# Squares and block sums of the first three groups of an MLP's first product: in halves, in one stretch, and in other places

## The chip, the cores and the metric

The kernel runs on one core of one Trainium2 chip. The metric is the device time of one execution in microseconds. Engines are named as in the profile: PE (TensorE, the matrix engine), DVE (VectorE), ACT (ScalarE), POOL (GpSimd) and SP (SyncE, which issues the DMAs here). Each engine works through its own instructions strictly in the order in which the program issued them; where one waits, all behind it wait.

## The reference

One pre-norm encoder block over 1024 tokens of width 1024. What matters here is its last part:

```
h = rms_norm(x, norm2_g) @ w_mlp_in          # 1024 -> 4096
x = x + square(relu(h)) @ w_mlp_out          # 4096 -> 1024
```

Ahead of it stand an input projection, neighbourhood attention, a gated short convolution and an output projection. All are float32.

## The kernel before, in words

Every float32 operand is split into a scaled float16 high part and a float16 low part, and every product is done in three passes (high x high, high x low, low x high). The larger products are done by Winograd's form of Strassen's method: of two 2x2 block matrices, seven block products instead of eight, with sums of blocks before and behind.

The first MLP product is cut into 16 *groups* (q = 0 to 15). A group takes 256 of the 4096 hidden columns, as two blocks of 128, and all 1024 tokens, as two blocks of 512; its result is a 2x2 of blocks of 128 partitions x 512. `quad(q, c0, c1)` does one group for the columns c0 to c1 of the 512. Groups 0 and 1 are done in halves, since the tokens of the second half (256 to 511) are normalized later: the order is `quad(0, 0, 256)`, `quad(1, 0, 256)`, `quad(0, 256, 512)`, `quad(1, 256, 512)`, then whole groups from 2 on.

A group is seven *units*, one for each block product, of 12 matmuls each (4 slices of the contraction x 3 passes). The order of the products is 1, 6, 5, 4, 2, 7, 3, and in the second halves 1, 2, 5, 4, 6, 7, 3. Each product goes to one of eight PSUM banks in turn. The tile `as` of a group has seven places z[0] to z[6] of 128 x 512 float32 and there are two such tiles, so group q + 2 reuses the tile of group q. What is done with the products ("sums of products"):

- product 1: ACT copies it to z[4] (L1475)
- product 6: z[5] = product 6 + z[4] on DVE (L1458)
- product 5: z[1] = product 5 - z[5] (L1463)
- product 2: z[0] = product 2 + z[4] (L1477)
- product 7: z[6], z[2], z[3] from products 7, 4 and 5 (L1466 to L1468)
- product 3: z[1] = product 3 + z[1] (L1471)

z[0] to z[3] are then the four blocks of h. `h_done(q)` finishes the group: ReLU on ACT over z[0:4] in place (L1432), scaled square in place with its maximum bound accumulated (L1434), four *block sums* by `sums` for the second MLP product (z[5], z[2], z[4], z[6] from z[0] to z[3]; L1159; on DVE for groups 0 and 1, on POOL from group 2 on), and the store of the whole tile to DRAM (L1438, queue `hs`). When the store has been issued, the group leaves `live`; `quad(q + 2)` steps the foreground until it has.

The order of the work on the engines is written out by the program as it is built, with generators. `unit` issues a unit's matmuls, then the sums of products of the unit *before* it (`settle`), and then advances generators: each `step()` advances every generator in the foreground list `fg` by one `yield`, each `tick()` the first one in the background list `bg`. A unit of a first half makes three steps, every other unit two, and each makes five ticks. `h_done(q)` is put into `fg` with the sums of product 3, so its first advance stands behind the first unit of the next group.

In the background the weights of the groups to come are prepared, one group after the other: rows scaled on ACT (L952), squares on ACT (L961), sums of blocks on POOL (L966); then, some units later, a sum over the squares and its cast on DVE (L932, L933), a one-column matmul with a matrix of ones on PE (L179), the scale from it on DVE (L182, L405 to L412), and the split into high parts on ACT (L981) and low parts on DVE (L977). For group q + 2 the one-column matmul stands behind the fourth unit of group q, and the splits behind its sixth.

`forms_m` splits the weights of group 1 by hand and puts parts of them where room is left; two of the places are the tiles `t2` and `t4` of 128 x 2 x 512 float16, read by group 1's products 6 and 4.

Of the kernel before, what the change touches and what calls it, by code (L numbers as in the profile page):

```python
# [10 lines left out]
F32 = mybir.dt.float32  # L11
# [3 lines left out]
AF = mybir.ActivationFunctionType  # L15
# [37 lines left out]
def encoder_block(ctx: ExitStack, tc: tile.TileContext, x, weights, cols, gqk, rel, masks, out):  # L53
    nc = tc.nc
    V, A, G, T, SP = nc.vector, nc.scalar, nc.gpsimd, nc.tensor, nc.sync
# [23 lines left out]
    sc = base.tile([128, 512], F32, name="sc")  # L79
# [3 lines left out]
    def cols_of(kind, n):  # L83
        a = area[kind]
        if a[1] + n > a[2]:
            assert kind != "keep"
            a[1] = a[0]
        a[1] += n
        return slice(a[1] - n, a[1])

    def keep(n=1):
        return cols_of("keep", n)

    def tmp(n=1):
        return cols_of("tmp", n)

    def at(c, i, n=1):
        return slice(c.start + i, c.start + i + n)
# [6 lines left out]
    def pow2(mx, top, s, inv, floor=True, more=0):  # L105

        if floor:
            V.tensor_scalar(sc[:, mx], sc[:, mx], 1e-30, None, op0=OP.max)
            yield
        V.tensor_scalar(sci[:, inv], sci[:, mx], EXP, None, op0=OP.bitwise_and)  # L110
        yield
        V.tensor_scalar(sci[:, s], sci[:, inv], -1.0, float((254 + top) << 23), op0=OP.mult, op1=OP.add)
        V.tensor_scalar(sci[:, inv], sci[:, inv], 1.0, float(-(top + more) * (1 << 23)), op0=OP.mult, op1=OP.add)
        yield


    fg, bg = [], []
# [9 lines left out]
    def step(n=1):  # L127
        for _ in range(n):
            for g in list(fg):
                if not advance(g):  # L130
                    fg.remove(g)
# [80 lines left out]
    def load_upto(n):  # L212
        while loaded[0] < min(n - held[0], limit[0], len(loads)):
            ch, p = loads[loaded[0]]
            loaded[0] += 1
            t = rawp.tile([128, 1024], F32, name="raw")
            load_into(t[:, :ch.widths[p][0] * ch.widths[p][1]], ch, p)
            ch.raw.append(t)
# [107 lines left out]
    for (kind, j), pieces in plan():  # L326
# [4 lines left out]
        for p, (k, w) in enumerate(ch.widths):  # L331
            ch.offs.append(offset)
            if kind != "X" and (kind, j) != ("1", 0) and (kind, j, p) != ("1", 1, 1):
# [3 lines left out]
    cV, cConv, cA, cB, cO, c1, c2, c2x = ([chunks[k, j] for j in range(n)] for k, n in  # L337
                                              (("V", 2), ("C", 4), ("A", 4), ("B", 4), ("O", 2),
                                               ("1", 16), ("2", 4), ("X", 4)))
# [205 lines left out]
    for p in range(11):  # L545
# [7 lines left out]
        for q in (p,) if p < 6 else (2 * p - 6, 2 * p - 5):  # L553
            c = q // 2 + 3
# [306 lines left out]
    for k in range(N + 15):  # L861
        p, w = k // 16, k % 16
# [147 lines left out]
    def seven(P, act, c0, c1, posts, steps, ticks, order=(1, 6, 5, 4, 2, 7, 3)):  # L1010

        ps = {}
        at_w = P if callable(P) else lambda w, i, k: P[:, w, i, k * 128:k * 128 + 128]
        for i in order:
            f, w = SEVEN[i]
            ps[i] = anybank()[:, c0:c1]
            post = posts.get(i)
            unit(group(ps[i], [(at_w(w, sw, k), act(f, sa, k)[:, c0:c1])
                               for k in range(4) for sw, sa in PASSES]),
                 post and (lambda post=post: post(ps)), steps, ticks)  # L1020
# [134 lines left out]
    def sums(f, sub):  # L1155

        z = [f[:, i] for i in range(7)]
        for o, a, b, op in ((5, 0, 2, OP.subtract), (2, 2, 3, OP.subtract), (4, 2, 0, OP.subtract), (6, 1, 4, OP.add)):
            sub.tensor_tensor(z[o], z[a], z[b], op=op)  # L1159
            yield  # L1160
# [27 lines left out]

    PART = ((0, 4), (4, 7))

    spare = []

    def pieces(n, part):

# [30 lines left out]
    def need(i):  # L1225
        while i not in ready:
            assert bg
            forced[0] = True
            tick()
            step()  # L1230
        forced[0] = False
# [51 lines left out]
    def forms_m():  # L1283

        (w11, w12), (w21, w22) = ([c1[1].raw[i].rearrange("p (n m) -> p n m", n=2)[:, j] for j in range(2)]
                                  for i in range(2))
        s = scaled[0]
        three = [rawp.tile([128, 1024], F32, name="raw").bitcast(F16).rearrange("p (f i c) -> p f i c", f=2, i=2)
                 for _ in range(3)]
        spare.extend(three[:2])  # L1290
        two = three[2]
        held[0], limit[0] = 3, c1[2].first + 1
        load_upto(done[0] + 5)
        t2 = w4p.tile([128, 2, 512], F16, name="t2", bufs=1)
        t4 = w4p.tile([128, 2, 512], F16, name="t4", bufs=1)
        k4 = lambda v: v.rearrange("p (k c) -> p k c", k=4)
        flat = {0: lambda i: P1[0][:, 7, i], 1: lambda i: two[:, 0, i], 2: lambda i: two[:, 1, i],
                5: lambda i: t2[:, i], 6: lambda i: t4[:, i]}

        def place(f, i):  # L1300
            return k4(flat[f](i)) if f in flat else M[0][:, 4 * (f - 3):4 * (f - 3) + 4, 512 * i:512 * i + 128]

        P1[1] = lambda f, i, k: place(f, i)[:, k]
        src = {0: w11, 1: w21, 2: w22, 3: w11, 4: w12, 5: w22, 6: w21}

        def hi(f):
            A.activation(place(f, 0), k4(src[f]), AF.Copy, scale=sc[:, s])

        def lo(f):
            V.scalar_tensor_tensor(place(f, 1), k4(src[f]), sc[:, s], place(f, 0), op0=OP.mult, op1=OP.subtract)  # L1310

        def add(o, a, b):
            V.tensor_tensor(o, a, b, op=OP.add)

        hi(0), hi(2), hi(1), lo(0), add(w11, w11, w12), lo(2)
        yield
        add(w12, w12, w22)
        yield
        add(w22, w22, w11), lo(1), hi(5), add(w21, w21, w22), hi(6)
        yield  # L1320
        lo(5), lo(6)
        yield
        hi(3), hi(4)
        yield
        lo(3)
        yield
        lo(4)
        done[0] += 1
        held[0], limit[0] = 1, c1[3].first
        load_upto(done[0] + 5)  # L1330
        ready.add(1)
# [16 lines left out]
    def wait(n):  # L1348
        for _ in range(n):
            yield  # L1350
# [17 lines left out]
    def tail(b, half, *acts):  # L1368
        proj(b, half, acts)
        for a in acts:  # L1370
            a()

    chain = forms_m()

    def sq(b, half=None):
# [48 lines left out]


    AS, live = {}, set()
    bsum, R = [keep(4) for _ in range(4)], [(keep(), keep()) for _ in range(4)]
    r_ready = [False] * 4

    def h_done(q):  # L1430
        f = AS.pop(q)
        A.activation(f[:, 0:4], f[:, 0:4], AF.Relu)  # L1432
        yield
        A.activation(f[:, 0:4], f[:, 0:4], AF.Square, scale=sc[:, c1[q].inv],  # L1434
                     accum_out=sc[:, at(bsum[q // 4], q % 4)])
        yield
        yield from sums(f, G if q > 1 else V)
        SP.dma_start(HS[q // 4][:, :, q % 4], f)  # L1438
        live.remove(q)
        if q % 4 == 3:  # L1440
            m = tmp()
            V.tensor_reduce(sc[:, m], sc[:, bsum[q // 4]], axis=AX, op=OP.max)
            yield
            yield from pow2(m, 14, *R[q // 4])
            r_ready[q // 4] = True

    def quad(q, c0=0, c1=512):
        need(q)
        if c0 == 0:
            while q - 2 in live:  # L1450
                step()
            live.add(q)
            AS[q] = w4p.tile([128, 7, 512], F32, name="as", tag="as")
        ps = {}
        z = [AS[q][:, i, c0:c1] for i in range(7)]

        def post6(ps):
            V.tensor_tensor(z[5], ps[6], z[4], op=OP.add)  # L1458
            if c0:
                post5(ps)  # L1460

        def post5(ps):
            V.tensor_tensor(z[1], ps[5], z[5], op=OP.subtract)  # L1463

        def post7(ps):
            V.tensor_tensor(z[6], ps[7], z[5], op=OP.add)  # L1466
            V.tensor_tensor(z[2], ps[4], z[6], op=OP.add)  # L1467
            V.tensor_tensor(z[3], ps[5], z[6], op=OP.subtract)  # L1468

        def post3(ps):  # L1470
            V.tensor_tensor(z[1], ps[3], z[1], op=OP.add)  # L1471
            if c1 == 512:
                fg.append(h_done(q))
        seven(P1[q], actU2, c0, c1, {
            1: lambda ps: A.activation(z[4], ps[1], AF.Copy),  # L1475
            6: post6, 5: None if c0 else post5,
            2: lambda ps: V.tensor_tensor(z[0], ps[2], z[4], op=OP.add),  # L1477
            7: post7, 3: post3}, 2 if c1 == 512 else 3, 5, (1, 2, 5, 4, 6, 7, 3) if c0 else (1, 6, 5, 4, 2, 7, 3))

    def whole(q):  # L1480
        quad(q)
        pe_done[0] = q + 1

    quad(0, 0, 256)
    quad(1, 0, 256)
    while pair_done[0] < 4:
        step()
# [131 lines left out]
    t2 = w5p.tile([128, 2, 1024], F32, name="t2")  # L1619
# [119 lines left out]
```

## Time and profile before

| | before |
|---|---|
| median of 3 timed runs | 1243.88 us (1243.17 to 1244.32) |
| profiled execution | 1241.45 us, span 1239.7 us |
| PE busy | 1200.9 us, 97% of the span |
| DVE, ACT, POOL busy | 930.0 (75%), 765.2 (62%), 425.5 us (34%) |
| granted TensorE clock, mean | 0.996 |
| first MLP product | from 645.75 us of the span |

The profile is of one execution. Its timelines give, for each engine, start and length of its instructions in us from the start of the span, the source line, the operation, out <- in by the program's names, the shapes, how many were merged, and in brackets the idle time of the engine before it with what ended it. Matmuls overlap, so a unit's row is a little longer than its distance to the next. The granted clock is the share of TensorE's full clock that it was allowed.

### The profile page before, as it was taken

The page shows a single profiled execution, that of the slowest core. Times are in us where ns is not written, and L with a number is a line of the kernel's source. Part 1 is how long each engine was busy: PE and PEld are TensorE (multiplying, and loading weights), DVE is VectorE, ACT ScalarE, POOL GpSimd, SP SyncE. Part 2 cuts the span into 40 slices and gives each one's busy share as a digit, 9 for nine tenths or more (in the row PEclk, how much of TensorE's full clock was granted, in tenths as well). Part 3 has the DMA queues.
Part 4 walks back from the last instruction along what each step waited for, and adds up shares of the span by engine and source line. Part 5 has one row for each costly group of instructions (what it writes and reads, how often), then busy time and mean ns, then how long its engine had stood idle before and what let it go on. Part 6 is the DMA issues. An engine that isn't in the chain of part 4 may idle for free.

```text
span 1239.7 us, 17066 instructions
## 1 busy us (share of the span) xinstructions
PE 1200.9 (97%) x6294; PEld 575.6 (46%) x6294; DVE 930.0 (75%) x1743; ACT 765.2 (62%) x1179; POOL 425.5 (34%) x289
## 2 busy tenths in 40 slices
PE   5989999999999999999999899999999999999998
PEld 3534444444444444444458344444444444444444
DVE  6668677988557777877877654564546999999997
ACT  6777577787474554536767877877765763645430
POOL 2440003111331111101003356556657473473562
PEclk8999999999999999999999999999999999999999
DMA  6557446656651211216096543553474744436202
GB/s 257 107 203 170 79 120 137 133 119 120 132 144 44 68 45 58 68 34 255 18 178 146 204 150 130 187 171 136 161 288 161 300 167 148 167 116 232 102 34 102
DMA packets 170868, 173.36 MB, mean 140 GB/s; under 512 B 131488, under 2 KB 132000, under 8 KB 166688
## 3 DMA queue, kind: packets, MB, share of 16 engines
q1 hardware_dynamic: 170784, 172.27, 47.0%
q8 instruction: 49, 0.80, 0.3%
q14 instruction: 35, 0.29, 0.1%
HBM read 102.51 MB, written 37.75 MB: 113 GB/s over the span
## 4 chain that ended last, share of the span: by engine, by line
PE 67%; DVE 18%; ACT 7%; issue 4%; DMA 1%; POOL 1%; SPq 0%; DVEq 0%; ACTq 0%; POOLq 0%
PE ps_d L188 26%; PE ps_s L188 20%; PE ps_o L188 18%; PE ps_d L859 3%; DVE sz L797 2%; DVE P L823 2%; DVE w_s L977 2%; DVE w_ws L278 1%; DVE ops L1572 1%; POOL sform L481 1%; DMA raw<-in_weights 1%; ACT w_ws L241 1%; ACT as L1432 1%; DVE sc L302 1%; DVE sg L1093 1%
## 5 line engine op out<-in xcount | busy, mean ns | idle before, releaser
L188 PEld LDWEIGHTS <-ops 128*128 128x128 f16 x1356 | 132.4, 98 | 159.5 <-issue 2.7
L188 PEld LDWEIGHTS <-w 128*128 128x128 f16 x1368 | 133.2, 98 | 145.7 <-issue 7.2
L859 PE MATMUL ps_d<-uT,w_ws 128*128 128x512 f16 x528 | 125.4, 379 | 0.0
L188 PE MATMUL ps_d<-ops 128*128 128x512 f16 (+1 forms) x528 | 118.4, 374 | 0.0
L188 PE MATMUL ps_s<-ops 128*128 128x512 f16 x492 | 113.2, 379 | 1.5 <-DVE ops L1572 1.1
L1563 ACT ACTIVATE ops<-hf,sc 128x2048 f16<-128x2048 f32 x26 | 52.0, 1998 | 93.7 <-PE ps_o L188 34.8
L966 POOL TENSOR_TENSOR tsum<-raw 128x512 f32<-128x512 f32 x28 | 45.5, 1637 | 156.5 <-ACT raw L952 145.8
L188 PEld LDWEIGHTS <-uT 128*128 128x128 f16 x648 | 65.0, 101 | 70.4 <-issue 5.6
L1159 POOL TENSOR_TENSOR as<-as 128x512 f32<-128x512 f32 x56 | 76.6, 1369 | 37.1 <-ACT as L1434 33.8
L188 PEld LDWEIGHTS <-w_s 128*128 128x128 f16 x588 | 56.8, 98 | 69.4 <-DVE w_s L977 1.9
L188 PE MATMUL ps_d<-u2x,w 128*128 128x512 f16 (+1 forms) x360 | 80.0, 372 | 0.0
L1565 DVE SCALAR_TENSOR_TENSOR ops<-hf,sc,ops 128x2048 f16<-128x2048 f32 x26 | 74.2, 2852 | 5.2 <-ACT ops L1563 5.2
L188 PE MATMUL ps_o<-ops 128*128 128x512 f16 x336 | 77.1, 379 | 0.0
L859 PEld LDWEIGHTS <-w_ws 128*128 128x128 f16 x528 | 50.8, 98 | 52.5
L188 PE MATMUL ps_o<-u2T,w 128*128 128x512 f16 (+1 forms) x324 | 71.7, 371 | 0.0
L952 ACT ACTIVATE raw<-raw,sc 128x256 f32<-128x256 f32 x172 | 70.8, 493 | 0.7 <-DMA raw<-in_weights 0.7
L966 POOL TENSOR_TENSOR gsum<-raw 128x512 f32<-128x512 f32 x14 | 18.9, 1371 | 131.7 <-issue 57.1
L981 ACT ACTIVATE w<-raw,sc 128x512 f16<-128x512 f32 (+1 forms) x28 | 24.6, 927 | 61.2 <-DVE sc L411 61.2
L188 PE MATMUL ps_s<-u2T,w 128*128 128x512 f16 (+1 forms) x252 | 54.2, 366 | 2.4 <-DVE as L1467 2.4
L1458 DVE TENSOR_TENSOR as<-ps_d,as 128x512 f32<-128x512 f32 (+1 forms) x15 | 10.1, 673 | 58.8 <-ACT as L1475 58.8
L806 ACT ACTIVATE sz<-sz,sc 128x384 f32<-128x384 f32 (+1 forms) x64 | 37.3, 582 | 26.9 <-DVE sc L797 13.5
L278 DVE SCALAR_TENSOR_TENSOR w_ws<-raw,sc,w_ws 128x512 f16<-128x512 f32 (+2 forms) x72 | 46.1, 690 | 2.4 <-ACT w_ws L291 2.4
(336 smaller groups left out, 2615.2 us busy)
## 6 DMA issues: line engine op xcount, KB each, us to landing
raw<-in_weights SPq DMA_DIRECT2D x89, 512.0 KB, 5.5
hs<-as SPq DMA_DIRECT2D x16, 1792.0 KB, 8.7
hf<-hs SPq DMA_DIRECT2D x26, 1024.0 KB, 6.5
w2x<-in_weights SPq DMA_DIRECT2D x16, 512.0 KB, 8.1
raw<-in_weights SPq DMA_DIRECT2D x16, 384.0 KB, 3.8
xt<-in_x SPq DMA_DIRECT2D x8, 512.0 KB, 9.9
gs<-s SPq DMA_DIRECT2D x4, 1024.0 KB, 6.2
x<-in_x SPq DMA_DIRECT2D x8, 512.0 KB, 10.0
```

The source lines that it names most:

```text
L188: T.matmul(ps, l, r, start=a, stop=b)
L278: V.scalar_tensor_tensor(lo, self.raw[p][:, o:o + m], sc[:, c:c + 1], hi, op0=OP.mult, op1=OP.subtract)
L797: V.tensor_tensor_reduce(z[:, :d["n"]], d["ps"][:, :d["n"]], bm, sc[:, cneg], 3.0e38, OP.add, OP.min, accum_out=sc[:, d["mx"]])
L806: A.activation(z, z, AF.Exp, scale=-1.0, bias=sc[:, d["mx"]], accum_out=sc[:, d["sm"]])
L823: V.scalar_tensor_tensor(d["lo"], d["z"][:, :d["n"]], sc[:, d["r"]], d["hi"], op0=OP.mult, op1=OP.subtract)
L859: T.matmul(ps, l, r, start=a, stop=b)
L952: A.activation(v, v, AF.Copy, scale=sc[:, at(g, 4 * i + k)])
L966: G.tensor_tensor(t[:, o], a, b, op=OP.add)
L977: V.scalar_tensor_tensor(o(1), w, sc[:, s], o(0), op0=OP.mult, op1=OP.subtract)
L1159: sub.tensor_tensor(z[o], z[a], z[b], op=op)
L1563: A.activation(P[:, 1, 0], hf, AF.Copy, scale=sc[:, Rs])
L1565: V.scalar_tensor_tensor(P[:, 1, 1], hf, sc[:, Rs], P[:, 1, 0], op0=OP.mult, op1=OP.subtract)
```

## The change

Groups 0, 1 and 2 are treated differently; from group 3 on nothing changes.

- `h_done` takes columns c0 to c1 and two counts of waits (each wait is one advance that does nothing), one ahead of ReLU and one ahead of the block sums.
- Group 0 runs `h_done` once for each half of the columns: for the first half with 3 and 24 waits, for the second with 3 and 4. Only the second issues the store. The first half's accumulated maximum gets a column of its own.
- Group 1 runs it once, whole, with 2 and 6 waits.
- For groups 0 and 1 the four block sums are issued on DVE in one advance, instead of one for each advance.
- Group 2 puts its z[4] and z[5] (product 1's copy and product 6's sum) into `t2` and `t4`, read as 128 x 512 float32, instead of into its own tile. Its block sums still write z[4] and z[5] of its tile.

```diff
-    spare = []
+    spare, extra = [], []
...
+        extra.extend(t.rearrange("p a c -> p (a c)").bitcast(F32) for t in (t2, t4))
...
-    bsum, R = [keep(4) for _ in range(4)], [(keep(), keep()) for _ in range(4)]
+    c1w = c1
+    bsum, R = [keep(4 if i else 5) for i in range(4)], [(keep(), keep()) for _ in range(4)]
...
-    def h_done(q):
-        f = AS.pop(q)
-        A.activation(f[:, 0:4], f[:, 0:4], AF.Relu)
-        yield
-        A.activation(f[:, 0:4], f[:, 0:4], AF.Square, scale=sc[:, c1[q].inv],
-                     accum_out=sc[:, at(bsum[q // 4], q % 4)])
-        yield
-        yield from sums(f, G if q > 1 else V)
+    def h_done(q, c0=0, c1=512, wait1=0, wait2=0):
+
+        f = AS[q] if c1 < 512 else AS.pop(q)
+        v = f[:, :, c0:c1]
+        yield from wait(wait1)
+        A.activation(v[:, 0:4], v[:, 0:4], AF.Relu)
+        yield
+        A.activation(v[:, 0:4], v[:, 0:4], AF.Square, scale=sc[:, c1w[q].inv],
+                     accum_out=sc[:, at(bsum[q // 4], 4 if c1 < 512 else q % 4)])
+        yield
+        yield from wait(wait2)
+        if q > 1:
+            yield from sums(v, G)
+        else:
+            for _ in sums(v, V):
+                pass
+        if c1 < 512:
+            return
         SP.dma_start(HS[q // 4][:, :, q % 4], f)
         live.remove(q)
...
         z = [AS[q][:, i, c0:c1] for i in range(7)]
+        if q == 2:
+            z[4:6] = extra
...
         def post3(ps):
             V.tensor_tensor(z[1], ps[3], z[1], op=OP.add)
-            if c1 == 512:
-                fg.append(h_done(q))
+            if q == 0:
+                fg.append(h_done(q, c0, c1, 3, 4 if c0 else 24))
+            elif c1 == 512:
+                fg.append(h_done(q, 0, c1, *((2, 6) if q == 1 else ())))
```

## The prediction

> **What bounds the kernel now.** I read the engine table and the slices first (TensorE, PE in the rows, is busy in nearly every slice), then the windows by stage, to find where it is not, and then the timelines of PE, VectorE (DVE) and ScalarE (ACT) around that place. In the windows the columns are the stretch, its length, the busy time of PE, of weight loads, DVE, ACT and POOL, then the granted TensorE clock, the DMA share and rate.
>
> ```profile
> 682.70:699.40 16.70, 12.36 (x50) 5.08 (x48) 9.96 (x21) 13.60 (x20) 5.09 (x4) 0.90 0.52 174
> ...
> 735.70:900.00 164.30, 164.30 (x771) 74.57 (x770) 89.77 (x187) 122.38 (x180) 99.86 (x74) 1.00 0.48 159
> ```
>
> From 735.7 to 900 PE has no gap. In the 16.7 us in which group 2 of the MLP's first product begins, it has 4.3 us of gaps and a granted clock of 0.90. This is the change's place, so the question is what stops PE there. Its timeline (start, length, what, count, then the idle time before it and who ended it):
>
> ```profile
> 677.42 0.17 PE L179 MATMUL ps_d<-ones 128*128 128x1 bf16 x1
> ...
> 682.69 2.75 PE L188 MATMUL ps_o<-u2T,w 128*128 128x512 f16 x12
> ...
> 690.39 4.23 PE L188 MATMUL ps_s<-u2T,w 128*128 128x512 f16 x12 [2.36 <-DVE as L1467]
> 694.41 3.00 PE L188 MATMUL ps_d<-u2T,w 128*128 128x512 f16 x12
> 699.42 0.16 PE L179 MATMUL ps_s<-ones 128*128 128x1 bf16 x1 [2.01 <-DVE ones L933]
> ...
> 707.21 2.75 PE L188 MATMUL ps_o<-u2T,w 128*128 128x512 f16 x12
> ...
> 717.57 0.17 PE L179 MATMUL ps_s<-ones 128*128 128x1 bf16 x1
> ```
>
> An undisturbed unit takes 2.59 us (707.21 to 717.57 holds four). Group 2 starts at 682.69, its third unit should start at 687.87 and starts at 690.39: 2.52 us lost. The third unit lasts to 694.41, 4.02 us instead of 2.59: 1.43 lost. The fourth ends at 697.00 and the one-column matmul behind it (the sum for group 4's weight scale) starts at 699.42: 2.42 lost. Together 6.37 us, 16.73 from 682.69 to 699.42 less four units.
>
> The 1.43 us are the clock:
>
> ```profile
> 690.40:693.00 2.60, 2.60 (x9) 1.02 (x9) 0.60 (x2) 2.57 (x5) 1.59 (x2) 0.71 0.74 287
> 693.00:695.00 2.00, 2.00 (x6) 0.72 (x5) 0.00 (x0) 1.97 (x2) 1.92 (x2) 0.52 0.00 0
> ```
>
> Group 2's third unit has the same twelve matmuls as any other, but at 0.71 and then 0.52 of the clock, right behind the first gap. The Trainium skill (TensorE: Matmul & The Clock Gate, the closing table on why this matters) says that the clock falls to half only behind idle gaps of about 3 us or more. The trace disagrees as far as it shows: the gap here was 2.5 us. I come back to this among the rivals.
>
> Who made PE wait? The DVE and ACT queues, each in program order:
>
> ```profile
> 673.69 0.42 DVE L1471 TENSOR_TENSOR as<-ps_s,as 128x256 f32<-128x256 f32 x1
> ...
> 679.35 1.42 DVE L1159 TENSOR_TENSOR as<-as 128x512 f32<-128x512 f32 x2 [3.58 <-ACT as L1434]
> ...
> 682.34 0.15 DVE L182 TENSOR_SCALAR sc<-ps_d 128x1 f32<-128x1 f32 x1
> ...
> 683.17 0.14 DVE L412 TENSOR_SCALAR sc<-sc 128x1 int32<-128x1 int32 x1
> ...
> 688.67 0.41 DVE L1458 TENSOR_TENSOR as<-ps_o,as 128x256 f32<-128x256 f32 x1
> ...
> 689.91 0.42 DVE L1467 TENSOR_TENSOR as<-ps_s,as 128x256 f32<-128x256 f32 x1
> 690.25 0.41 DVE L1468 TENSOR_TENSOR as<-ps_s,as 128x256 f32<-128x256 f32 x1
> ...
> 696.50 1.42 DVE L1159 TENSOR_TENSOR as<-as 128x512 f32<-128x512 f32 x2 [5.50 <-ACT as L1434]
> ...
> 699.21 0.16 DVE L933 CAST ones<-sc 128x1 bf16<-128x1 f32 x1
> ```
>
> ```profile
> 660.25 0.36 ACT L1475 ACTIVATE as<-ps_d 128x256 f32<-128x256 f32 x1
> 665.05 1.76 ACT L981 ACTIVATE w<-raw,sc 128x512 f16<-128x512 f32 x2 [4.44 <-DVE sc L411]
> ...
> 674.24 1.06 ACT L961 ACTIVATE tsum<-raw 128x1024 f32<-128x1024 f32 x1
> 675.20 0.19 ACT L961 ACTIVATION_READ_ACCUMULATOR tsum<-raw 128x1 f32 x1
> 675.30 1.89 ACT L1432 ACTIVATE as<-as 128x2048 f32<-128x2048 f32 x1
> 677.22 2.00 ACT L1434 ACTIVATE as<-as,sc 128x2048 f32<-128x2048 f32 x1
> ...
> 692.45 1.89 ACT L1432 ACTIVATE as<-as 128x2048 f32<-128x2048 f32 x1
> ```
>
> First gap: ACT does ReLU and square of the whole of group 0 (L1432, L1434) from 675.30 to about 679.3. DVE stands still 3.58 us for it, to 679.35, with group 0's sums (L1159) at the head of its queue; behind them the scale of group 3's weights (L182 to L412), its splits, and only then group 1's sums of products (L1458 at 688.67 to L1468 at 690.25). PE's third unit needs a bank that these read. Second gap: ACT comes to ReLU and square of group 1 only at 692.45, DVE stands 5.50 us with group 1's sums at its head until 696.50, and behind these stands L933 (699.21), which the one-column matmul needs. Both gaps are thus one thing: L1159 at the head of DVE's queue, waiting for a square that ACT hasn't done.
>
> **The change part by part.** A generator in the foreground list advances three times behind each unit of a first half, twice behind every other unit; a unit's sums of products are issued behind the next unit's matmuls.
>
> *Group 0, columns 0 to 255.* The generator now starts behind the first half's last product, in group 1's first-half unit 1. Three waits put its ReLU and square behind group 1's unit 2, which on ACT is behind the copy at 660.25. ACT is then free from 660.6 until 665.05 (4.44 us in the row). Cost: the trace has no half-wide square of this kind; the nearest row is the 128x1024 square of the weights (1.06 and 0.19 for the accumulator). I take 1.0 for the ReLU and 1.25 for the square. The lower bound is half the full ones, the upper the full 1.89 + 2.00 + 0.19: even this, begun at 660.6, ends at 664.7. So hidden: nothing on the path, at either end. The 24 waits put the sums at step 30, 21 of them in group 1's first half, nine in group 0's second: behind its unit 5, ahead of its sums for products 6, 7 and 3. Four sums of 256 columns at 0.34 to 0.45 between starts (the half-wide rows 689.91 and 690.25) are 1.6 us; the full ones are 0.66 apart (1.42 for two), an upper bound of 2.7. L1471 moves from 673.69 to about 674.5; its end is needed by ReLU of the second half, which comes later than that anyway. Cost nothing; at the upper bound about 1 us of slack is used.
>
> *Group 0, columns 256 to 511.* ReLU is now behind group 1's second-half unit 2, so the copy of product 1 goes ahead of it. ACT: weights' squares to 675.39, copy (0.36) to 675.75, ReLU to 676.75, square to 678.0 (before: 679.3). DVE: the scale of group 3 no longer stands behind the sums. Its L182 can follow the end of the one-column matmul, 677.42 + 0.17, and L182 to the end of L412 takes 0.97 (682.34 to 683.31): 678.6. Then the half sums, 1.6: 680.2. The store of group 0 goes to SP's queue here, at about 680.3; the two weight loads behind it there stay behind it.
>
> ```profile
> 702.24 0.69 DVE L1477 TENSOR_TENSOR as<-ps_o,as 128x512 f32<-128x512 f32 x1 [0.79 <-PE ps_o L188]
> 702.84 1.94 DVE L977 SCALAR_TENSOR_TENSOR w<-raw,sc,w 128x512 f16<-128x512 f32 x2
> ...
> 707.09 0.68 DVE L1466 TENSOR_TENSOR as<-ps_d,as 128x512 f32<-128x512 f32 x1
> ...
> 709.01 0.68 DVE L1471 TENSOR_TENSOR as<-ps_s,as 128x512 f32<-128x512 f32 x1
> ...
> 715.12 0.69 DVE L1458 TENSOR_TENSOR as<-ps_d,as 128x512 f32<-128x512 f32 x1 [5.42 <-ACT as L1475]
> ...
> 715.90 0.16 DVE L933 CAST ones<-sc 128x1 bf16<-128x1 f32 x1
> ```
>
> The splits (L977) take 4.25 us where nothing holds them (702.84 to 707.09): 684.5. From L1458 to the end of L1468 it was 1.99: 686.5. PE wants the bank at 687.87. The first gap is gone with 1.4 us to spare, and with it the low clock. Were both the squares and the sums as dear as full ones, some 1 us of gap would stay.
>
> *Group 2's products 1 and 6 in other places; group 1's squares later.* Product 1's copy and product 6's sum go into the two small tiles, which PE last reads in group 1's units 4 and 5, so neither waits for group 0's store. The first write into the tile itself is product 5's, which DVE can do when the third unit has ended, at 682.69 + 3 x 2.59 + 0.16 = 690.6 (a unit's row is 0.16 longer than its distance to the next).
>
> ```profile
> 682.50 0.62 SPq L1438 DMA_DIRECT2D hs<-as  x1
> ...
> hs<-as SPq DMA_DIRECT2D x16, 1792.0 KB, 8.7
> ```
>
> The store took 8.7 us from issue to landing; issued at 680.3 it lands at 689.0, 1.6 us before that. The two waits put group 1's ReLU behind the copy of product 1 instead of ahead of it. ACT runs weight splits, row scaling and weight squares of one group in 9.16 us when fed:
>
> ```profile
> 701.42 1.76 ACT L981 ACTIVATE w<-raw,sc 128x512 f16<-128x512 f32 x2 [4.47 <-DVE sc L411]
> ...
> 710.58 1.89 ACT L1432 ACTIVATE as<-as 128x2048 f32<-128x2048 f32 x1
> ...
> 714.51 0.58 ACT L1475 ACTIVATE as<-ps_o 128x512 f32<-128x512 f32 x1
> ```
>
> (701.42 to 710.58.) Begun at 678.6, that ends at 687.8; copy to 688.4; L933 ended 0.94 behind the start of DVE's sum for product 6 (715.12 to 716.06): 689.4. PE reaches the one-column matmul at 682.69 + 4 x 2.59 = 693.05. The second gap is gone with 3.6 us to spare. Sum so far: all of the 6.37.
>
> *What it costs.* Six waits put group 1's sums, four in one stretch, behind product 2's sum in group 2's sixth unit. The fifth unit ends at 695.8, product 2's sum takes 0.60 to the next start (702.24 to 702.84), and four sums at 0.66 are 2.65 (bounds 2.4 to 2.9, at 0.60 and 0.72): 699.1. Behind them are queued the splits of group 4 (4.25, to 703.3) and group 2's products 7 and 3 (707.09 to 709.69 took 2.60: 705.9). Who waits: group 2's ReLU on ACT. ACT had otherwise been ready: group 4's scale is done at 693.05 + 0.17 + 0.97 = 694.2, and 9.16 later it is 703.4. So ReLU starts at 706.0 and product 1's copy of group 3 3.93 later (710.58 to 714.51): 709.9. L933 followed the copy by 1.39 (715.90) and PE followed L933 by 0.21 (699.21, 699.42): 711.5. PE arrives at 682.69 + 11 x 2.59 = 711.2. A new gap of 0.3 us; a quarter group later the loop has its old slack again (715.90 + 0.21 against 717.57: 1.46 us).
>
> The store of group 1 is now issued at 699.1, lands at 707.8, and group 3's first write, the copy at 709.9, waits no longer than ReLU makes it.
>
> **Sum.** 6.37 - 0.3 = 6.0 us (estimate). Behind it, to 900, PE alone sets the pace and everything is issued relative to it, so the whole moves forward. The profiled execution took 1241.45 with a span of 1239.7; it becomes 1235.4. The timed runs' median is 2.43 higher, 1243.88: 1237.9.
>
> **The rivals.**
>
> *A. A real gap in group 3 (0.17).* For it: the 0.3 us stands on a chain of six estimated ends. If DVE ends 1.5 us later (four sums at 0.72 and the splits slowed), the gap is 1.8 us; with a clock drop like the one above, 1.43 more. Gain 6.37 - 3.2 = 3.1: 1240.7. Against: the copies and splits have durations from rows.
>
> *B. The low clock has another cause than the gap and stays (0.05).* Then 4.6 are gained: 1239.3. For it: the second gap, 2.42 long, was followed by no drop:
>
> ```profile
> 699.40:702.00 2.60, 2.58 (x13) 1.19 (x13) 1.91 (x8) 0.58 (x1) 0.00 (x0) 1.00 0.30 112
> ```
>
> Against: from 735.7 to 900 the same units run at 1.00 without a gap, and the only low clock of this stage stands behind the first gap. By the Trainium skill's page named above, gaps this short do nothing to the clock; that is this rival.
>
> *C. Given back (0.08).* If the later stage, where DVE is busier and PE has small waits, were paced by something that doesn't move with PE (loads, stores), the end would stay: within 2.5 us of 1243.88. Against: 164.3 us of PE without a gap lie between, and loads are issued by splits done.
>
> *D. Slower (0.08).* The mechanism: the tile of group 3 waits for group 1's store, whose issue now stands two units nearer to its use (behind the sixth unit instead of the fourth). The copy on ACT then waits at the head, and behind it group 5's work and, one for one, L933. It decides from a landing past 709.9; it costs more than it brings from a landing past about 716, 17 us behind the issue, and with a clock drop from about 714.5. A landing at 720 gives 10.4 + 1.4 lost against 6.37 won: 1249.3. For it: the slack is only 2 us, and two loads share the engines. Against: the median landing of this row is 8.7 with such loads behind it already.
>
> **How the numbers follow.** The forecast itself has 0.62: 1237.9. The best case is all 6.37 and the spread of the timed runs (0.7 below their median): 1236.8. The upper end takes in B and A to a gain of 2.6: 1241.3. C and D, 0.16, lie outside. Faster by over 0.2% (2.5 us, about what a measurement of this kernel can tell) is the forecast, A and B: 0.84; C is same, 0.08; D slower, 0.08.
>
> **What would show it.** Right: two ACT pairs of ReLU and square of 128x1024 for group 0, the first at about 661; its half sums on DVE at about 671 and 679, with no DVE idle time put down to L1434; group 2's first four units 2.59 apart at clock 1.00, the one-column matmul at about 693.1; the store of group 0 issued near 680.3; at most a gap of some 0.3 us ahead of the matmul at 711. Wrong: PE waiting for product 7's sums in group 2 or 3 for over 1 us; ACT's copy of group 3's product 1 put down to a store; the clock under 1.00 anywhere from 683 to 720; or gaps after 900 that grow by what was won.

## The result and the profile after

| | before | after |
|---|---|---|
| median of 17 timed runs each | 1243.52 us (1241.81 to 1246.13) | 1241.22 us (1239.74 to 1242.84) |
| ratio, with its 95% interval | | 0.9981 (0.9974 to 0.9989) |
| profiled execution, span | 1241.45, 1239.7 us | 1239.75, 1238.0 us |

The change gains 2.3 us, 0.19%; a gain of 6.0 had been forecast, with a time between 1236.8 and 1241.3. In the changed kernel's timeline of PE (the columns as before: start, length, what, count, idle time and who ended it), group 2 runs as forecast and the loss sits one group later:

```profile
665.63 1.48 PE L188 MATMUL ps_d<-u2T,w 128*128 128x256 f16 x12 [0.96 <-DMA u2T<-v]
...
684.01 2.75 PE L188 MATMUL ps_o<-u2T,w 128*128 128x512 f16 x12
...
689.19 2.75 PE L188 MATMUL ps_s<-u2T,w 128*128 128x512 f16 x12
...
694.37 0.17 PE L179 MATMUL ps_s<-ones 128*128 128x1 bf16 x1
...
702.16 2.75 PE L188 MATMUL ps_o<-u2T,w 128*128 128x512 f16 x12
...
716.05 0.16 PE L179 MATMUL ps_s<-ones 128*128 128x1 bf16 x1 [3.37 <-DVE ones L933]
```

From 684.01 to 694.37 are 10.36 us, four units of 2.59: both gaps of group 2, and the low clock, are gone (6.37 us). Group 3 starts at 702.16 and its one-column matmul should come at 712.52; it comes at 716.05, 3.53 us late, and again L933 on DVE ended the wait. (The idle time in brackets, 3.37, counts from the end of the row before, which is 0.16 later than the unit's distance.) Ahead of group 0's second half PE also waits 0.96 us for a transpose. DVE shows why group 3 is late:

```profile
671.16 2.80 DVE L1159 TENSOR_TENSOR as<-as 128x256 f32<-128x256 f32 x4
...
679.86 1.79 DVE L1159 TENSOR_TENSOR as<-as 128x256 f32<-128x256 f32 x4
...
687.40 0.41 DVE L1482 TENSOR_TENSOR as<-ps_s,as 128x256 f32<-128x256 f32 x1
...
690.49 0.16 DVE L933 CAST ones<-sc 128x1 bf16<-128x1 f32 x1
...
697.79 2.86 DVE L1159 TENSOR_TENSOR as<-as 128x512 f32<-128x512 f32 x4
700.57 2.96 DVE L977 SCALAR_TENSOR_TENSOR w<-raw,sc,w 128x512 f16<-128x512 f32 x2
703.45 4.49 DVE L977 SCALAR_TENSOR_TENSOR w<-tsum,sc,w 128x1024 f16<-128x1024 f32 x2
707.86 0.68 DVE L1480 TENSOR_TENSOR as<-ps_d,t 128x512 f32<-128x512 f32 x1
...
709.78 0.68 DVE L1485 TENSOR_TENSOR as<-ps_s,as 128x512 f32<-128x512 f32 x1
715.05 0.69 DVE L1472 TENSOR_TENSOR as<-ps_d,as 128x512 f32<-128x512 f32 x1 [4.59 <-ACT as L1491]
...
715.84 0.16 DVE L933 CAST ones<-sc 128x1 bf16<-128x1 f32 x1
```

The four sums of group 1 (697.79) are over at 700.57, where the forecast, moved by the 1.32 us by which group 2 starts later, had 700.4. But the splits behind them (L977) last from 700.57 to 707.86: 7.29 us, not 4.25. All behind them is 3 us late: ReLU of group 2 on ACT, product 1's copy, L933. Here are ACT and POOL, which is busy at the same time with the sums of blocks for group 5's weights (L966):

```profile
660.92 1.05 ACT L1437 ACTIVATE as<-as 128x1024 f32<-128x1024 f32 x1
662.00 1.15 ACT L1439 ACTIVATE as<-as,sc 128x1024 f32<-128x1024 f32 x1
...
710.50 1.91 ACT L1437 ACTIVATE as<-as 128x2048 f32<-128x2048 f32 x1 [5.69 <-DVE as L1485]
```

```profile
701.07 1.38 POOL L966 TENSOR_TENSOR tsum<-raw 128x512 f32<-128x512 f32 x1 [9.11 <-ACT raw L952]
702.67 1.99 POOL L966 TENSOR_TENSOR tsum<-raw 128x512 f32<-128x512 f32 x1 [0.23 <-ACT raw L952]
704.95 4.12 POOL L966 TENSOR_TENSOR tsum<-tsum,raw 128x512 f32<-128x512 f32 x2 [0.30 <-ACT tsum L961]
```

In the kernel before, the same splits ran from 702.84 to 707.09 and POOL's four sums came behind them:

```profile
706.93 1.38 POOL L966 TENSOR_TENSOR tsum<-raw 128x512 f32<-128x512 f32 x1 [11.63 <-ACT raw L952]
708.53 1.28 POOL L966 TENSOR_TENSOR tsum<-raw 128x512 f32<-128x512 f32 x1 [0.22 <-ACT raw L952]
710.82 2.63 POOL L966 TENSOR_TENSOR tsum<-tsum,raw 128x512 f32<-128x512 f32 x2 [1.01 <-ACT tsum L961]
```

Now they lie side by side, and both are slower: the last two of POOL's sums take 4.12 us instead of 2.63.

### The profile page after: what moved, and what is told of

The parts are those of the page before. It is cut to its first block, busy times and chain, and to the rows that moved or that the text cites. A ratio compares the mean times of both kernels' runs of the same rounds, so it can differ in the third digit from the quotient of the medians.

```text
span 1238.0 us, 17072 instructions
## 1 busy us (share of the span) xinstructions
PE 1199.7 (97%) x6294; PEld 575.1 (46%) x6294; DVE 932.7 (75%) x1747; ACT 767.0 (62%) x1182; POOL 429.4 (35%) x289
## 4 chain that ended last, share of the span: by engine, by line
PE 67%; DVE 19%; ACT 6%; issue 4%; DMA 2%; POOL 1%; SPq 0%; DVEq 0%; ACTq 0%; POOLq 0%
PE ps_d L188 26%; PE ps_s L188 20%; PE ps_o L188 18%; PE ps_d L859 3%; DVE sz L797 2%; DVE P L823 2%; DVE w_s L977 2%; DVE w_ws L278 1%; DMA xt<-in_x 1%; DVE ops L1588 1%; POOL sform L481 1%; DVE w L977 1%; ACT w_ws L241 1%; DMA u2T<-v 1%; DVE sg L1093 1%
## 5 line engine op out<-in xcount | busy, mean ns | idle before, releaser
L966 POOL TENSOR_TENSOR tsum<-raw 128x512 f32<-128x512 f32 x28 | 46.7, 1684 | 148.3 <-ACT raw L952 148.3
L966 POOL TENSOR_TENSOR gsum<-raw 128x512 f32<-128x512 f32 x14 | 19.0, 1377 | 131.7 <-issue 57.1
```

The costliest lines, as they stand in the source:

```text
L966: G.tensor_tensor(t[:, o], a, b, op=OP.add)
```

## The experiments

The theory after the two traces: DVE's splits and POOL's sums slow each other when they run together, and the change moved the one under the other. The rivals: the place of group 1's four sums makes the gap by itself; the store and the weight loads slow the splits; one of the three parts of the change is at fault. The ratios below are to the kernel before, on the same chip, with 95% intervals. In these kernels line numbers behind the edit are shifted by a few.

### Group 1's sums two units earlier

```diff
-                fg.append(h_done(q, 0, c1, *((2, 6) if q == 1 else ())))
+                fg.append(h_done(q, 0, c1, *((2, 2) if q == 1 else ())))
```

> The changed kernel with group 1's block sums two units earlier: 2 and 2 waits instead of 2 and 6, so that they stand on DVE behind product 5's sum of group 2 and ahead of group 4's scale. Contention theory (DVE's splits of group 4 and POOL's sums of group 5's weights slow each other when they run at the same time: 4.25 us became 7.3): the splits come ahead of POOL's sums again, take 4.3 to 4.7 us, PE's gap of 3.5 us in group 3 is gone; 3.5 us less than the changed kernel, ratio to before about 0.995 (1237.7). Rival, DMA traffic (the store and the weight loads slow the splits): the store is issued earlier still and lies over the splits, they stay near 7 us, a gap of over 2 us stays, ratio about 0.998.

Measured: 1235.47 us, 0.994 (0.9926 to 0.9953). DVE's splits of group 4:

```profile
697.61 0.75 DVE L977 SCALAR_TENSOR_TENSOR w<-raw,sc,w 128x512 f16<-128x512 f32 x1
698.65 1.29 DVE L977 SCALAR_TENSOR_TENSOR w<-raw,sc,w 128x1024 f16<-128x1024 f32 x1 [0.29 <-ACT w L981]
699.85 2.48 DVE L977 SCALAR_TENSOR_TENSOR w<-tsum,sc,w 128x1024 f16<-128x1024 f32 x2
702.24 0.69 DVE L1480 TENSOR_TENSOR as<-ps_d,t 128x512 f32<-128x512 f32 x1
```

They take 4.63 us, counted as the 4.25 and 7.29 were, to the start of the instruction behind them; 0.29 of it is a wait for ACT. PE has no gap in groups 2 and 3. The store, issued at 696.38 and so lying over the splits, does not slow them, which speaks against the traffic. By the ratios the gain over the changed kernel is about 5 us, more than the 3.5 of the gap. The clock, below, is the likely rest; that is an inference, since the two profiled executions are only 4.0 us apart.

### POOL held back, DVE's order untouched

```diff
+        if ch is c1[5]:
+            last = P1[4][:, 6, 1]
+            G.tensor_tensor(sc[:, tmp()], last[:, 510:511], last[:, 511:512], op=OP.add)
         for o, a, b in ((0, w11, w12), (1, w12, w22), (2, t[:, 0], w22), (3, t[:, 2], w21)):
             G.tensor_tensor(t[:, o], a, b, op=OP.add)
```

> The changed kernel, DVE's order untouched; one POOL instruction of one column that reads the last low part of group 4's weights is put ahead of POOL's sums of group 5's weights, so POOL starts these only when DVE has ended the splits. Contention theory: the splits take 4.3 us instead of 7.3, PE's gap ahead of the one-column matmul in group 3 falls from 3.5 to 0.4-0.8 us; ratio to before about 0.9955. Rivals, place alone (the four sums at the head of DVE's queue make the gap) or DMA traffic: splits near 7 us and a gap of 3 to 3.5 us stay, ratio 0.998.

Measured: 1236.08 us, 0.9946 (0.9933 to 0.9958). DVE, then POOL, then PE's one-column matmul in group 3:

```profile
699.45 1.94 DVE L980 SCALAR_TENSOR_TENSOR w<-raw,sc,w 128x512 f16<-128x512 f32 x2
701.31 2.47 DVE L980 SCALAR_TENSOR_TENSOR w<-tsum,sc,w 128x1024 f16<-128x1024 f32 x2
703.70 0.68 DVE L1483 TENSOR_TENSOR as<-ps_d,t 128x512 f32<-128x512 f32 x1
```

```profile
703.86 0.20 POOL L967 TENSOR_TENSOR sc<-w 128x1 f32<-128x1 f16 x1 [13.03 <-DVE w L980]
704.01 2.50 POOL L969 TENSOR_TENSOR tsum<-raw 128x512 f32<-128x512 f32 x2
706.47 2.62 POOL L969 TENSOR_TENSOR tsum<-tsum,raw 128x512 f32<-128x512 f32 x2
```

```profile
711.88 0.16 PE L179 MATMUL ps_s<-ones 128*128 128x1 bf16 x1 [0.32 <-DVE ones L933]
```

This decides it. Every DVE instruction stands where the changed kernel has it, the four sums included, and with POOL out of the way the splits are back at 4.25 us (699.45 to 703.70) and the gap at 0.48 us by the count that gave 3.53 (group 3 starts at 701.04 here; the row's idle time is 0.32). The prediction had 0.3. The store and the weight loads are issued from 699.91 on here, again over the splits. The run also shows what does not collide: from 704.0 on POOL's sums run beside DVE's sums for product 7 and 3 (L1466 to L1471 of the kernel before), and these keep their 0.68 us and POOL its 1.25 each. Those read one operand from PSUM; the splits and the block sums read two tensors from SBUF. The Trainium skill (GPSIMD Engine Reference, section 1, Specifications) states just this: POOL shares its SBUF interfaces with DVE and contends with DVE instructions that have two SBUF inputs. The trace agrees, and gives the size: 7.29 us against 4.25 for the splits, 2.06 against 1.31 for one of POOL's last two sums.

### Group 1's sums on POOL

```diff
-        if q > 1:
+        if q > 0:
             yield from sums(v, G)
...
-                fg.append(h_done(q, 0, c1, *((2, 6) if q == 1 else ())))
+                fg.append(h_done(q, 0, c1, *((2, 0) if q == 1 else ())))
```

> The changed kernel with group 1's block sums on POOL, behind its square, as from group 2 on. Contention theory: POOL is done with them at about 699, DVE's splits of group 4 start 2.9 us earlier, about 697.8, and end at 702.5 to 703.5, before or just as POOL starts group 5's sums; the gap in group 3 falls from 3.5 to 0-0.5 us; ratio 0.994 to 0.995. Rival (the gap hangs on something else in the change, such as group 1's late store): a gap of over 2 us stays, ratio 0.998.

Measured: 1235.52 us, 0.9946 (0.9932 to 0.9959), no gap in groups 2 and 3.

```profile
697.32 2.93 DVE L977 SCALAR_TENSOR_TENSOR w<-raw,sc,w 128x512 f16<-128x512 f32 x2
700.17 3.48 DVE L977 SCALAR_TENSOR_TENSOR w<-tsum,sc,w 128x1024 f16<-128x1024 f32 x2
```

The splits start where expected but take 6.3 us, since POOL's sums are beside them at both ends. They still end at 703.65, 3.8 us earlier than in the changed kernel (707.94), counted from the start of group 2 (683.53 here, 684.01 there): that is enough. So what counts is when the splits end, not that they are undisturbed.

### The parts alone

Group 0's halves alone:

```diff
-        if q == 2:
-            z[4:6] = extra
...
-                fg.append(h_done(q, 0, c1, *((2, 6) if q == 1 else ())))
+                fg.append(h_done(q, 0, c1))
```

> One part alone: group 0 in halves as in the changed kernel; group 1 without waits (its ReLU and square ahead of group 2's product 1 copy, its four sums in one advance behind the square), group 2 wholly in its own tile. Theory: the first gap (2.5 us and 1.4 us of low clock) is gone, the second stays at about 3 us (one-column matmul of group 4 at 697.4 instead of 694.4), none in group 3; ratio about 0.997, better than the whole change. Rival (the parts work only together): the first gap stays, ratio 1.000.

Measured: 1238.61 us, 0.9968 (0.9955 to 0.998): by the ratio more than the whole change brings (0.9981), though the two intervals overlap a little. The first gap is gone, the second stays:

```profile
696.41 0.16 PE L179 MATMUL ps_s<-ones 128*128 128x1 bf16 x1 [2.39 <-DVE ones L933]
```

Its splits meet POOL's sums, too:

```profile
703.37 4.51 DVE L977 SCALAR_TENSOR_TENSOR w<-tsum,sc,w 128x1024 f16<-128x1024 f32 x2
```

But PE comes later by the second gap and by 1.7 us of low clock behind it, and nothing waits for the splits in group 3.

Group 1's waits and group 2's places alone, with group 0 whole:

```diff
-    bsum, R = [keep(4 if i else 5) for i in range(4)], [(keep(), keep()) for _ in range(4)]
+    bsum, R = [keep(4) for i in range(4)], [(keep(), keep()) for _ in range(4)]
...
-            if q == 0:
-                fg.append(h_done(q, c0, c1, 3, 4 if c0 else 24))
-            elif c1 == 512:
+            if c1 == 512:
```

> The second and third part alone: group 0 whole, its ReLU and square at once behind its last product as before, its sums in one advance; group 1 with 2 and 6 waits and group 2 in the small tiles as in the changed kernel. Theory: the first gap (2.5 us and low clock) stays, the second is gone, and a new one of 2.5 to 3.5 us stands in group 3 with splits of near 7 us beside POOL's sums; nothing won, ratio 0.999 to 1.002. Rival (the parts add up: this one removes 2.4 us whatever the other does): ratio 0.998.

Measured: 1243.9 us, 1.0009 (1.0 to 1.0018).

```profile
690.75 2.75 PE L188 MATMUL ps_s<-u2T,w 128*128 128x512 f16 x12 [2.07 <-DVE as L1481]
...
717.61 0.16 PE L179 MATMUL ps_s<-ones 128*128 128x1 bf16 x1 [3.37 <-DVE ones L933]
```

The first gap stays, the second is gone, and a gap as long as that of the changed kernel stands in group 3. This part of the change takes 2.4 us away and puts 3.5 there; so what the change gains comes from the halves.

Group 2 back in its own tile, all else as in the change:

```diff
-        if q == 2:
-            z[4:6] = extra
```

> The changed kernel without its third part: group 2 writes product 1's copy and product 6's sum into its own tile. Theory (that part brings nothing, since ACT comes to the copy at 689.1 and the store lands at about 690.4): ACT waits about 1.3 us, all of it slack, PE's timeline as in the changed kernel within 0.5 us; ratio 0.998. Rival (that part carries the gain in group 2): PE waits over 1 us at group 2's one-column matmul, ratio 0.9995 or more.

Measured: 1240.72 us, 0.9983 (0.9974 to 0.9991), the changed kernel's value. The places in `t2` and `t4` bring nothing that can be measured: without them ACT's copy of product 1 waits 1.04 us for the store of group 0, and PE does not wait for the copy. The profiled execution of this kernel was 3 us longer than the changed kernel's, though, and the clock is the reason.

### What a gap costs besides itself

PE of the kernel with group 2 in its own tile, and its windows behind the gap (stretch, length, busy time of PE, weight loads, DVE, ACT, POOL, then clock and DMA):

```profile
716.07 0.16 PE L179 MATMUL ps_s<-ones 128*128 128x1 bf16 x1 [3.37 <-DVE ones L933]
716.09 5.28 PE L188 MATMUL ps_o<-u2T,w 128*128 128x512 f16 x12
721.16 3.21 PE L188 MATMUL ps_d<-u2x,w 128*128 128x512 f16 x12
```

```profile
716.00:718.00 2.00, 1.94 (x6) 0.73 (x6) 1.34 (x8) 0.55 (x1) 1.92 (x2) 0.50 0.00 0
718.00:720.00 2.00, 2.00 (x6) 0.72 (x5) 0.00 (x0) 2.00 (x3) 1.87 (x2) 0.50 0.00 0
720.00:722.00 2.00, 2.00 (x6) 0.64 (x5) 0.59 (x1) 2.00 (x5) 0.00 (x0) 0.50 0.43 163
```

and the changed kernel's:

```profile
716.00:718.00 2.00, 1.95 (x10) 0.90 (x10) 1.33 (x7) 0.56 (x1) 1.92 (x2) 1.00 0.00 0
```

The same gap of 3.37 us, ended by the same instruction at the same time: in one execution the clock falls to half and the next unit takes 5.07 us instead of 2.59, with 0.46 more on the one behind it; in the other the clock stays at 1.00. The timed runs of this kernel go the same way: 1239.08 and 1239.17 us at a mean clock of 0.997, 1242.07 and 1242.41 at 0.993; the mean does not say in which place the clock was lost. The group 1 part alone, with gaps of 2.07 and 3.37, lost no clock in its profiled execution (1241.28 us, mean clock 0.997), while its other timed runs reach 1247.15 at 0.993. Behind its 2.39 us the halves alone had 0.54:

```profile
696.40:699.00 2.60, 2.59 (x8) 1.03 (x8) 1.29 (x7) 1.20 (x2) 0.00 (x0) 0.54 0.76 284
```

The ten profiles show it once more at a place that the change doesn't touch. Ahead of some matmuls near 64.5 us PE waits 2.34 to 2.38 us for a load in every one of them. In three (the changed kernel, the halves alone, group 1's sums on POOL) the clock then falls to between 0.57 and 0.75 from 64 to 68, and in the other seven it stays at 1.00. There the drop costs next to nothing: 24 matmuls take 1.7 us longer, and PE then waits that much less for DVE.

So a gap brings a chance of a slow stretch, and one costs 1.4 to 3 us where PE sets the pace. The Trainium skill (TensorE: Matmul & The Clock Gate, Part 1) says that the window in which the activity is counted runs freely and isn't tied to the program; the spread agrees. The rule in the closing table of that page, no gaps over about 3 us, does not hold here in either direction: 2.34 us was followed by a drop, 3.37 us was not.

A second profile of the kernel before was to show this, too:

> The kernel before, profiled a second time, for what differs between executions of one program. Clock theory (how much a gap of PE costs depends on where it lies against a window that isn't tied to the program): the two gaps of 2.5 and 2.4 us in group 2 stand again within 0.3 us, the loss of clock behind them differs from the 1.4 us of the first profile by over 0.5 us, up to two drops; the wait for the transpose ahead of group 0's second half is 0.2-0.4 us again if the halves cause the 0.6-1.0 us seen with them, and differs if not. Rival (the first profile is typical): the same low clock behind the first gap alone, 1.3 to 1.5 us.

```profile
691.20 4.44 PE L188 MATMUL ps_s<-u2T,w 128*128 128x512 f16 x12 [2.39 <-DVE as L1467]
695.47 2.75 PE L188 MATMUL ps_d<-u2T,w 128*128 128x512 f16 x12
700.24 0.16 PE L179 MATMUL ps_s<-ones 128*128 128x1 bf16 x1 [2.01 <-DVE ones L933]
```

It did not: 1.68 us of lost clock (691.20 to 695.47, less 2.59), behind the first gap only, much like the first profile. The rival (1.3 to 1.5) came nearer than the theory (a difference of over 0.5). The wait for the transpose was 0.34 us, within the 0.2 to 0.4 expected. That the timed runs of the kernel before lose more than its profiled ones is an inference: these executions took 1241.45 and 1242.11 us, below the median of 1243.52, and the kernel without gaps gains 7.5 us by its ratio of 0.994, where the gaps and the clock of the profile make 6.4.

### The wait for the transpose

```diff
-                fg.append(h_done(q, c0, c1, 3, 4 if c0 else 24))
+                fg.append(h_done(q, c0, c1, *((3, 4) if c0 else (23, 4))))
```

This is on top of the kernel with group 1's sums two units earlier.

> e1_early_sums with the first half's ReLU and square of group 0 behind group 0's second-half product 1 copy (23 waits instead of 3, 4 instead of 24), so that ACT writes nothing while the last transposes run. Theory A (ACT's work there slows the transposes): PE's wait for the transpose falls from 0.9 to 0.2-0.4 us, no new gap, 0.5 us less than e1, ratio 0.9935. Theory B (that wait varies from one execution to the next by itself): 0.5-1.0 us stays, ratio 0.994.

Measured: 1235.45 us, 0.9944 (0.9932 to 0.9957). PE's waits from 640 us on with the early first half (in us: total, number, longest):

```profile
PE ps_s L188 <- DVE ops L1588: 1.1, 2, 0.8
PE ps_d L188 <- DMA u2T<-v: 0.9, 1, 0.9
PE ps_s L188 <- DVE as L1493: 0.5, 1, 0.5
```

With the late one the list has the first and the third line as they stand, and the wait for the transpose is gone. The transpose itself, from issue to landing, took 9.1 us with the early first half and 8.3 with the late one. All six profiles in which the first half's ReLU and square stand at 661 show the wait, at 0.55 to 0.96 us; the four without have 0.34 or less. The profiled executions are 0.5 us apart, but the medians are the same, 1235.45 and 1235.47: what the wait is worth in time could not be measured, and how ACT's work delays the transposes stays open.

Four versions are the fastest: this one, its parent, the one with group 1's sums on POOL and the one with POOL held back. By the ratios (0.994 to 0.9946 against 0.9981) all four beat the changed kernel by 4 to 5 us.

## Why the prediction was wrong

**The place and the mechanism of the gain in group 2 were right.** The first gap went as the steps said: halves hidden on ACT at 661 (1.05 and 1.34 us, forecast 1.0 and 1.25), half sums of 1.79 us at 679.86, the bank free at 687.8 with 1.4 us to spare ahead of 689.19. The second went too, L933 ending at 690.65 for a matmul at 694.37.

**The step that failed is a term of the cost: "the splits of group 4 (4.25, to 703.3)".** They took 7.29. The 4.25 came from a row in which POOL was idle, and the order of ACT, DVE and PE was followed into group 3 without POOL's. With POOL held back they took 4.25 again and the gap was 0.48 us, so the rest of that chain of sums was right. The row that warned was in POOL's timeline of the kernel before: a sum of POOL that took 2.43 us instead of 1.27 beside a DVE subtraction of two tensors from SBUF. Here is DVE's row, then POOL's:

```profile
657.43 2.05 DVE L1207 TENSOR_TENSOR v<-form,v 128x1536 f16<-128x1536 f32 x1
```

```profile
658.20 2.43 POOL L966 TENSOR_TENSOR tsum<-raw 128x512 f32<-128x512 f32 x1 [0.33 <-ACT raw L952]
```

With 3.04 us more, the forecast gap of 0.3 becomes 3.3; measured 3.53. A second sum missed POOL in the same way, without harm: the first half's four block sums, put at 1.6 us with an upper bound of 2.7, took 2.80 (671.16), and DVE had the slack. They took 1.79 in the four kernels in which POOL's sums start only about as they end. Rival A had the place and the kind, "a real gap in group 3", but let DVE end 1.5 us later at most and gave it 0.17.

**That the time lies inside the range is luck.** The median of 1241.22 is 0.08 us below the upper end, 1241.3, which stood for a gain of 2.6 from 1243.88. The gain was 2.3; the time came out inside because the median of the kernel before was 1243.52 over 17 runs, 0.36 lower than over the first three. Rival A comes to a similar gain, 3.1, by a gap of 1.8 us and a drop of the clock behind it; in the profiled execution the gap was 3.53 us and no drop followed.

**The clock.** The forecast took 1.43 us, from one execution, as a fixed price. It is a chance: the gap left in group 3 costs 3.5 us in one execution and 6.5 in another. In the changed kernel's profiled execution no clock was lost there, and its sum comes out: 6.37 won, less 3.53, less 0.93 for the transpose (PE came 1.12 us late there, 0.19 before the change), less 0.40 by which the MLP began later, is 1.51; the span shrank by 1.7.

**The transpose** was not among the terms. "Cost nothing" for the first half holds for the queues and misses this 0.9 us in the trace.

**Rivals.** B (the low clock stays without a gap) fell: in the profiled groups 2 and 3 of the kernels without gaps no clock is lost. C (given back later) fell too: what groups 2 and 3 win reaches the end in the four kernels without a gap of over 0.5 us there: their one-column matmul of group 3 comes 5.5 to 6.1 us earlier than in the kernel before (717.57), their end 5.7 to 6.3 us earlier. D (the late store of group 1) did not show: ACT's copy waits for ReLU, which waits for DVE (5.69 us before 710.50).

## What to carry to other kernels

When a step is moved on one engine, lay the moved time over every other engine's work, not only over those that it waits for: a duration from a row holds for the neighbours that this row had. Order DVE instructions with two SBUF inputs and POOL's so that they alternate, or put beside POOL what reads PSUM. A gap of TensorE of 2 to 3.5 us cost its length here and, in some executions only, 1.4 to 3 us of low clock besides. One profile shows one draw of that, so a gap removed may gain more in the median than the profile says, and a gap added may cost more.

## What the runs showed of the hardware that was not expected

- DVE's splits (128x512 and 128x1024 to float16) go from 4.25 to 7.29 us beside POOL's float32 sums, these from 1.31 to 2.06 us each; DVE's four block sums of 256 columns from 1.79 to 2.80 us (679.86, POOL idle, and 671.16, POOL busy). DVE sums with a PSUM operand beside POOL: 0.68 us, unchanged.
- The granted clock can fall to half behind gaps of 2.4 us, and can stay at 1.00 behind 3.4 us; behind one and the same gap of 2.34 to 2.38 us it fell in three of ten executions. A drop cost 1.4 to 3 us where PE set the pace, and next to nothing where PE waited for DVE behind it.
- With 2.4 us of ACT work beside the last transposes, PE waits 0.55 to 0.96 us for what they bring, without it 0.34 or less (six profiles and four). The cause is open.
